# A streaming-encoder block on one core: squares of h reloaded from DRAM, second-product loads ahead of the last stores, next x through four buffers

## Chip, cores and metric

The kernel runs on one core of one Trainium2 chip. The metric is the device time in microseconds (us) of one execution; the time of a kernel is the median of its runs.

## The reference

One layer on x of 2048 rows and 1024 columns, all in float32:

```python
hn   = rmsnorm(h, norm_mix_w)                 # h = x
proj = hn @ w_in                              # 1024 x 4112: q, k, v, z, xbc, dt
h    = h + concat[attention(q,k,v), ssd(z,xbc,dt)] @ w_out
hn   = rmsnorm(h, norm_mlp_w)
h    = h + square(relu(hn @ w_ff1)) @ w_ff2   # D_FF = 4096
y    = rmsnorm(h, norm_final_w)
# ssd: silu(causal conv of xbc), dt = softplus(dt_raw + dt_bias), chunked scan
# of the heads with decay exp(cumsum(-exp(a_log) * dt)), gate silu(z), grouped rmsnorm
```

## The kernel before, in words

The columns of the transposed activations are rows of the sequence. They are worked through in two **halves** of 1024, the first half (`hf` 0) from projection to output, then the second. Every float32 product is made of three matmuls of rounded halves (`mm3`, L245): a tile is split by ACT into a rounded high part (L229) and by DVE into the rest (L230); high x high, high x low and low x high are added in PSUM.

A half goes through these stages:

- **Input projection**, in units of the list `gm` (class `Gemms`, L62): unit dt (L347, 16 columns with the small weight tile `wd`), the convolution units conv0, conv1, ... (24 column blocks by `in_proj`, L332), z, q, k, v. `dt_chain` (L825) turns dt into the decays: eight transposes on PE (L831), `dt_u` (L833), a series on DVE (L843 to L850), `at` (L855), and then, in a second step, a matmul over `at` (L859).
- **SSD scan and attention**, with projection units as filler.
- **Output projection**: units `u_wo_y` (L513), then the four units `u_wo_a` (L534), called **woa** here. Each has 48 matmuls for two of the eight 128-row blocks d. Its reader adds the product to h (L556), forms from two blocks the seven sums and differences of the Strassen-Winograd scheme (`xB11`, `xT1`, `xT2`, `xB22`, `xT3`, `xB21`, `xT4`, L558 to L574), each as a high and a low tile, stores h to `h_d` in DRAM, and squares h on ACT in halves of 512 columns, which DVE adds up in `hacc` (L577 to L583).
- **ff1** (L624): 16 steps mp; each has seven products P1 to P7 of 12 matmuls, named in the order `ORD1` = P1, P6, P5, P7, P2, P3, P4. Step mp 0 first does three quarters (`range(3)`) of the first four products. The weights of a step are loaded, combined (`sum_a`, L587) and split by `Step1` (L598). The reader squares the result and stores seven sums to `f_d` (L680).
- **ff2** (L684): 28 products q of 48 matmuls (the order `ORD2` = P5, P6, P3, ...). `load_w` loads blocks A11, A21, A22, A12 of the weights (1 MB each), `load_a` sums of `f_d`; `split_w` and `split_a` combine and split them. The last products' outputs are scaled with the row norms by `last_rows` (L1065), whose DVE part is 16 operations at L1078.
- **Next half** (L1213 to L1240, `hf` 0 only): the eight blocks of the other half's x are loaded (L178), scaled by `rx` (L1222) and split (L1223); then `load_wd`, the dt unit, the norm rows, conv0, the first step of `dt_chain`, conv1.

**What sets the order.** PE runs in program order, as the code emits its matmuls. On the other engines a scheduler orders the instructions. SP issues all large DMAs, one after the other, and waits at an issue until its tile is free or its data are there; what stands behind it waits too. `stream` (L175, tiles `strm`) and `w_load` (L232, tiles `wraw`) have two buffers each:

```python
t   = wp.tile(list(shape), F, name=name, tag="strm", bufs=2)
raw = wp.tile([P, 8, P], F, name="wraw", tag="wraw", bufs=2)
```

In the rows, `mf` is the PSUM tile of woa and ff2, `fb` that of ff1, `mm` and `mw` those of the input projection, `sB` that of small sums; `w` and `w2h`/`wl` are split weights of ff1 and ff2, `ah`/`al` the split sums of ff2, `st` the tile that is stored to `f_d`.

Of the kernel before, what the change touches and what calls it, by code (L numbers as in the profile page):

```python
# [58 lines left out]
FREED = (6, 0, 2, 1, 4, 5, 7, 3)  # L59
# [91 lines left out]
def hymba(ctx, tc, xT, win, wdt, wout, w1, w2, par, rel, out):  # L151
# [382 lines left out]
    def u_wo_a(s, dd):  # L534

        def fn(wh, wl):
            hs_, X = [], {n: (s.X[n][0][:, dd, :], s.X[n][1][:, dd, :]) for n in s.X}

            def tmp(name):
                return s.mp.tile([P, 512], F, name=name, tag="xt", bufs=6)  # L540
# [3 lines left out]
            for z in range(2):  # L544
# [10 lines left out]
                for b in (1, 0) if z else (0, 1):  # L555
                    dve.tensor_tensor(hx[:, bsl(b)], p_[:, b, :], hx[:, bsl(b)], op=ALU.add)  # L556
# [30 lines left out]
    def sum_a(n, o, v):  # L587
# [4 lines left out]
        o = {"S1": o, "S2": v.get("S1"), "S3": v["A21"], "S4": v.get("S2")}[n]  # L592
# [3 lines left out]
    class Step1:  # L596
# [13 lines left out]
        def split(self, n):  # L610
            if n[0] == "S":
                sum_a(n, self.s.fw.tile([P, 512], F, name="s1", tag="s1", bufs=2) if n == "S1" else None, self.v)
            if n not in self.t:
                self.tile(n)
            split(*parts(self.t[n]), self.v[n])
# [8 lines left out]
    def ff1(s, w, nw):  # L624

        for mp in range(16):
# [25 lines left out]
            for k, p in enumerate(ORD1):  # L652
# [23 lines left out]
                else:  # L676
                    dve.tensor_tensor(a21, b, u, op=ALU.add)
                    square(a21, a21)
                    dve.tensor_tensor(t4, a21, t2, op=ALU.subtract)
            sp.dma_start(f_d[s.hf, mp // 4, :, :, mp % 4, :].rearrange("i p n -> p i n"), st[:, 0:7, :])  # L680
            w, nw = nw, nnw
            yield mp

    def ff2(s):  # L684
# [4 lines left out]
        def load_w(c, n):  # L689
# [3 lines left out]
            sp.dma_start(vs[c][n], w2[c, BLK.index(n)])  # L693

        def split_w(q):
            if q < len(order):
                c, p = order[q]
                n = PA[p]
                if n[0] == "S":
                    sum_a(n, s.f2.tile([P, 4, 512], F, name="ws", tag="ws", bufs=1) if n == "S1" else None, vs[c])  # L700
                lo = s.f2.tile([P, 4, 512], R, name="wl", tag="wl", bufs=2)
                his = [w_tile("w2h").rearrange("p (a b) c -> p a (b c)", a=2) for _ in range(2)]
                for g in range(2):
                    dps = slice(2 * g, 2 * g + 2)
                    split(his[g], lo[:, dps, :], vs[c][n][:, dps, :])
                ws[q] = his, lo

        def load_a(q):
            if q < len(order):
                c, p = order[q]  # L710
                t = s.f2.tile([P, 4, 512], R, name="al", tag="al", bufs=3)
                sp.dma_start(t.bitcast(F), f_d[s.hf, c, SUMS[PB[p]]])
                aa[q] = [None, t]

        def split_a(q):
            if q < len(order):
                aa[q][0] = s.f2.tile([P, 4, 512], R, name="ah", tag="ah", bufs=2)
                split(*aa[q], aa[q][1].bitcast(F))
# [5 lines left out]
        for n in ("A11", "A21", "A22", "A12"):  # L724
            load_w(0, n)
            if n == "A11":
                load_a(0)
        split_w(0)
        split_a(0)
        load_a(1)  # L730
        bank = {}
        for q, (c, p) in enumerate(order):
# [5 lines left out]
            if c < 3:  # L738
                for n in {0: BLK[:1], 3: BLK[1:2], 5: BLK[2:]}.get(k, ()):
                    load_w(c + 1, n)  # L740
            ah, al = aa[q]
            for g in range(2):
# [4 lines left out]
                for z in range(2):  # L747
                    for _ in mm3(b[:, z, :], [(wh[:, z, bsl(j, P)], wl[:, z, bsl(j, P)], ah[:, j, :], al[:, j, :])
                                              for j in range(4)], p not in ON, True, p in ON):
                        pass  # L750
# [332 lines left out]
    def mixer(s):  # L1083
# [38 lines left out]
        s.es_xr, s.xr = open_pool(f"xr{s.hf}", "right")  # L1122
# [5 lines left out]

# [256 lines left out]
```

## Time and profile before

| | |
|---|---|
| time, median of 3 runs | 2803.35 us (2801.03 to 2804.41) |
| profiled execution, its own time | 2804.53 us |
| its span | 2802.8 us |
| PE busy | 2610.8 us (93%), 12398 matmuls |
| DVE busy | 2031.2 us (72%) |
| ACT busy | 1348.3 us (48%) |
| mean granted clock of PE | 0.966 |

The span is what the profiler saw from the first to the last instruction; the rest of the execution's own time lies around it. The clock is a share of full speed, so a stretch at 0.50 runs at 1.2 GHz in place of 2.4 GHz. A timeline row gives the start, the busy time, engine, line and operation, and in brackets how long the engine had been idle and what ended that; `x8` counts merged instructions, whose time is then that of the row together.

### The profile page before, as it was taken

Reading aid. Unit: us, or ns where it says so; the run is one execution under the profiler, and the core shown is the slowest. Engines: PE = TensorE matmul, PEld = TensorE weight load, DVE = VectorE, ACT = ScalarE, POOL = GpSimd, SP = SyncE. Lnnn points to the kernel's source line nnn. Section 1 sums busy time; section 2 is a strip of 40 time slices with the busy share of each in tenths; the row PEclk is TensorE's granted clock in tenths of the full one; section 3 lists DMA queues with packets and bytes.
Section 4 is the critical chain, followed back from the end, with each engine's and each line's share of the span. In section 5 each row is a group of like instructions: output and inputs, shape, how many; then the busy total and the mean of one; then the engine's idle time right before and its main releaser. Section 6 shows DMA issues by size and latency. Waiting matters only on the chain.

```text
span 2802.8 us, 32189 instructions
## 1 busy us (share of the span) xinstructions
PE 2610.8 (93%) x12398; PEld 2137.2 (76%) x12398; DVE 2031.2 (72%) x2866; ACT 1348.3 (48%) x2097; POOL 6.9 (0%) x42
## 2 busy tenths in 40 slices
PE   7999999999799978999599999999997999889997
PEld 4788778788588867888478877887885888668885
DVE  6797777756776646877767887778568666468877
ACT  5565456634554544433336554666335455344332
POOL 0000000000000000000000000000000000000000
PEclk9999999999899998999789999999998999989998
DMA  3232222334354355443332232113343434355432
GB/s 137 87 113 81 97 94 65 115 119 175 136 189 159 142 185 195 174 159 118 105 115 94 87 124 107 55 55 104 110 171 123 164 138 151 137 215 184 161 109 87
DMA packets 121450, 359.98 MB, mean 128 GB/s; under 512 B 10192, under 2 KB 27088, under 8 KB 110032
## 3 DMA queue, kind: packets, MB, share of 16 engines
q1 hardware_dynamic: 121296, 357.93, 36.1%
q8 instruction: 97, 1.59, 0.2%
q14 instruction: 57, 0.47, 0.1%
HBM read 257.09 MB, written 100.79 MB: 128 GB/s over the span
## 4 chain that ended last, share of the span: by engine, by line
PE 81%; DVE 10%; DMA 4%; ACT 2%; issue 1%; SPq 0%; DVEq 0%; ACTq 0%
PE mm L251 25%; PE fb L251 22%; PE mf L251 21%; PE sB L1020 3%; PE mw L251 2%; PE S L977 2%; PE tp L1002 2%; DMA w<-in_w 1%; PE yp L927 1%; PE sB L936 1%; PE yp L925 1%; DMA strm<-h_d 1%; PE mm L356 1%; DMA bias<-in_rel 1%; DVE wlo L230 1%
## 5 line engine op out<-in xcount | busy, mean ns | idle before, releaser
L251 PE MATMUL mm<-x,whi 128*128 128x512 f32 x2304 | 745.1, 405 | 1.4 <-ACT u L372 0.6
L251 PEld LDWEIGHTS mm<-x,whi 128*128 128x128 f32 x2304 | 417.7, 189 | 88.3 <-issue 14.4
L251 PE MATMUL mm<-x,wlo 128*128 128x512 f32 x1152 | 453.1, 393 | 0.0
L251 PE MATMUL mf<-ah,w2h 128*128 128x512 f32 x896 | 351.3, 392 | 47.7 <-ACT w2h L229 47.7
L251 PE MATMUL mf<-ah,wl 128*128 128x512 f32 x896 | 351.1, 392 | 2.3 <-DVE wl L230 2.3
L251 PE MATMUL mf<-al,w2h 128*128 128x512 f32 x896 | 351.0, 392 | 1.9 <-DVE al L230 1.9
L251 PEld LDWEIGHTS mm<-x,wlo 128*128 128x128 f32 x1152 | 217.3, 189 | 48.2
L251 PEld LDWEIGHTS mf<-ah,w2h 128*128 128x128 f32 x896 | 169.7, 189 | 83.6 <-ACT w2h L229 48.6
L251 PEld LDWEIGHTS mf<-ah,wl 128*128 128x128 f32 x896 | 169.4, 189 | 39.1 <-DVE wl L230 3.7
L251 PEld LDWEIGHTS mf<-al,w2h 128*128 128x128 f32 x896 | 169.7, 189 | 38.1 <-DVE al L230 2.7
L988 ACT ACTIVATE pt<-pt,mx 128x640 f32<-128x640 f32 (+4 forms) x128 | 97.6, 762 | 161.7 <-DVE mx L986 161.1
L229 ACT ACTIVATE ah<-al 128x2048 fp32r<-128x2048 f32 x56 | 106.8, 1908 | 132.6 <-PE mf L251 103.6
L230 DVE TENSOR_TENSOR al<-al,ah 128x2048 fp32r<-128x2048 f32 x56 | 127.9, 2284 | 39.5 <-ACT ah L229 39.5
L229 ACT ACTIVATE w<-wraw 128x512 fp32r<-128x512 f32 x128 | 80.2, 630 | 149.7 <-PE fb L251 142.4
L229 ACT ACTIVATE whi<-wraw 128x1024 fp32r<-128x1024 f32 x88 | 92.8, 1054 | 120.0 <-PE mm L251 86.8
L230 DVE TENSOR_TENSOR wlo<-wraw,whi 128x1024 fp32r<-128x1024 f32 x88 | 107.5, 1222 | 45.5 <-ACT whi L229 40.7
L251 PE MATMUL fb<-xT2h,w 128*128 128x512 f32 x256 | 87.3, 401 | 35.7 <-ACT w L229 35.7
L230 DVE TENSOR_TENSOR w<-s,w 128x512 fp32r<-128x512 f32 x96 | 66.1, 689 | 70.0 <-ACT w L229 68.9
L760 DVE TENSOR_TENSOR acc<-mf,acc 128x1024 f32<-128x1024 f32 x64 | 77.9, 1219 | 53.1 <-PE mf L251 52.9
L986 DVE CUSTOM_DVE_ANT_0 pt<-S,bias 128x640 f32<-128x640 f32 (+4 forms) x128 | 94.1, 735 | 30.4 <-PE S L977 29.8
L892 ACT ACTIVATE csb<-csb,cst 128x128 f32<-128x128 f32 x256 | 79.2, 389 | 70.1 <-DMA csb<-cs_d 70.1
L229 ACT ACTIVATE w2h<-w 128x1024 fp32r<-128x1024 f32 x64 | 65.3, 1054 | 92.3 <-PE mf L251 80.1
(297 smaller groups left out, 5316.6 us busy)
## 6 DMA issues: line engine op xcount, KB each, us to landing
f_d<-st SPq DMA_DIRECT2D x32, 1792.0 KB, 6.2
al<-f_d SPq DMA_DIRECT2D x56, 1024.0 KB, 4.8
wraw<-in_win SPq DMA_DIRECT2D x64, 512.0 KB, 3.3
wraw<-in_w SPq DMA_DIRECT2D x64, 512.0 KB, 3.2
w<-in_w SPq DMA_DIRECT2D x32, 1024.0 KB, 4.8
strm<-in_xT SPq DMA_DIRECT2D x32, 512.0 KB, 4.4
csb<-cs_d SPq DMA_DIRECT2D x32, 512.0 KB, 3.9
h_d<-strm SPq DMA_DIRECT2D x32, 512.0 KB, 2.6
```

The source lines that it names most:

```text
L229: act.activation(hi, raw, AF.Copy)
L230: dve.tensor_tensor(lo, raw, hi.bitcast(F), op=ALU.subtract)
L251: pe.matmul(ps, a, b, start=(first and i == 0), stop=(last and i == n - 1), skip_group_check=on)
L356: pe.matmul(ps[b][:48, pc], s.wd[:, kt, :], x_[kt][:, c], start=(kt == 0 and x_ is s.xh), stop=(kt == NKT - 1 and x_ is s.xl))
L760: dve.tensor_tensor(o, b, o, op=ALU.add)
L892: act.activation(E[:, h, :], E[:, h, :], AF.Relu, scale=-1.0, bias=s.cst[:, k:k + 1])
L925: pe.matmul(yo[:, j, :], S[:, bsl(j, P)], Cf[:, ch], start=True, stop=True)
L977: pe.matmul(S[:, a, 0:w], q[p][hd][:, bsl(lb, P)], s.ks[p][hd][:, k0 + st:k0 + st + w], start=(z == 0), stop=(z == 1))
L986: dve.tensor_tensor_reduce(out=o_, in0=s_, in1=b_, scale=1.0, scalar=1e30, op0=ALU.add, op1=ALU.min, accum_out=mx)
L988: act.activation(pt[:, 0:n], pt[:, 0:n], AF.Exp, scale=-1.0, bias=mx, accum_out=sm)
L1002: pe.transpose(tp[:, bsl(c, P)], pt[:, bsl(c, P)], ident)
L1020: pe.matmul(pv[:, i0 * P:(i1 + 1) * P], lhsT, rhs, start=(z == 0), stop=(z == 2 * len(order) - 1))
```

## The change

1. **Squares of h.** woa no longer squares h. In ff1, steps mp 0 to 3 reload two blocks of `h_d` each through `stream`; ACT squares 128x1024, DVE adds up in `ra` (`squares_of`). The mean and the row norms move from mp 0 to mp 5 and 6, the next half's x squares from one block in each of mp 4 to 11 to two in each of mp 7 to 10, `rx` from mp 13 to 12. The addition to h (L556) is one 128x1024 operation except in the last block.
2. **First weights of ff1.** Four of the seven `step`s of the first `Step1` are emitted ahead of the end of woa, three just behind it; one tile `s1` in place of two; temporaries of woa 5 in place of 6; all seven sums in one pool on the left.
3. **First loads of ff2.** They are emitted in mp 15 of ff1 ahead of its last store to `f_d` (the pool of ff2 is opened there). The first product's loads, sums, splits and matmuls are done in two halves along the contraction.
4. **Next half.** Odd blocks of x come through `wraw`, even ones through `strm`; `load_wd` and the first splits of conv0's weights are emitted during ff2. The dt unit, conv0 and conv1 are woven: for each block of x two dt matmuls, three of conv0, three of conv1, for both groups of 512 columns in turn (`weave(3)`). `dt_chain` starts behind conv1.

```diff
 def u_wo_a(s, dd):                                  # woa
-                for b in (1, 0) if z else (0, 1):
-                    dve.tensor_tensor(hx[:, bsl(b)], p_[:, b, :], hx[:, bsl(b)], op=ALU.add)
+                for b in (1, 0) if d == 7 else (slice(0, 2),):
+                    o = hx.rearrange("p (a b) -> p a b", a=2)[:, b]
+                    dve.tensor_tensor(o, p_[:, b], o, op=ALU.add)
...
-                for b in range(2):
-                    c = bsl(b)
-                    if d == 0:
-                        act.activation(s.hacc[:, c], hx[:, c], AF.Square)
-                    else:
-                        sq = tmp("hsq")
-                        act.activation(sq, hx[:, c], AF.Square)
-                        dve.tensor_tensor(s.hacc[:, c], s.hacc[:, c], sq, op=ALU.add)
 def ff1(s, w, nw):
+            yield mp
             sp.dma_start(f_d[s.hf, mp // 4, :, :, mp % 4, :].rearrange("i p n -> p i n"), st[:, 0:7, :])
             w, nw = nw, nnw
-            yield mp
 def ff2(s):
-        for n in ("A11", "A21", "A22", "A12"):
-            load_w(0, n)
-            if n == "A11":
-                load_a(0)
...
+        for h in (slice(0, 2), slice(2, 4)):
+            load_w(0, "A21", h)
+            load_w(0, "A22", h)
+            load_a(0, h)
+        load_w(0, "A11")
+        load_w(0, "A12")
         split_w(0)
         split_a(0)
         load_a(1)
+        yield
...
+                for js in (range(4),) if q else (range(2), range(2, 4)):
+                    for z in range(2):
 def mlp(s):
         w.load(1)
+        for k in range(4):
+            w.step(k)
         until(s, "woa")
+        for k in range(4, 7):
+            w.step(k)
+            if k in (4, 6):
+                nw.load(k // 6)
...
+        def squares_of(src, kt):
+
+            hx = stream(src)
+            act.activation(hx if kt else ra, hx, AF.Square)
+            if kt:
+                dve.tensor_tensor(ra, ra, hx, op=ALU.add)
+
         for mp in ff1(s, w, nw):
-            if mp == 0:
-                means(sums_f(s, s.hacc), s.v)
+            if mp < 4:
+                for kt in (2 * mp, 2 * mp + 1):
+                    squares_of(h_d[s.hf, kt], kt)
+            elif mp == 5:
+                means(sums_f(s, ra), s.v)
...
+            elif mp == 15:
+
+                s.es_xx.close()
+                s.es_g, s.f2 = open_pool(f"f2{s.hf}", "left")
+                products = ff2(s)
+                next(products)
...
             for kt in range(NKT):
-                xr = stream(xT[kt * P:(kt + 1) * P, TH:2 * TH])
+                src = xT[kt * P:(kt + 1) * P, TH:2 * TH]
+                xr = w_load(src.rearrange("p (a b) -> p a b", b=P)).rearrange("p a b -> p (a b)") if kt % 2 else stream(src)
...
-            for _ in range(NKT):
-                gm.step()
+            products = gm.weave(3)
+            for _ in range(NKT + 1):
+                next(products)
             for r in rows:
                 next(r)
-            until(n, "dt")
+            for _ in products:
+                pass
             for r in rows:
                 for _ in r:
                     pass
-            gm.hold()
             n.chain = dt_chain(n)
             next(n.chain)
-            gm.hold()
```

**DVE at the end of woa, first half.** Before, from the last unit's first addition to h (L556) to the first combined weights of ff1 (L593; `w` and `s` with numbers are weight tiles, `t` and `b` temporaries):

```order
811 L556 TENSOR_TENSOR strm<-mf,strm 128x512 x2
812 L560 TENSOR_TENSOR t_5964<-strm 128x512
813 L556 TENSOR_TENSOR strm<-mf,strm 128x512 x2
814 L267 SCALAR_TENSOR_TENSOR xB11l<-strm,pr,xB11h 128x512
815 L583 TENSOR_TENSOR v<-v,hsq 128x512 x2
...
820 L583 TENSOR_TENSOR v<-v,hsq 128x512 x2
821 L230 TENSOR_TENSOR xT2l<-t_6005,xT2h 128x512
822 L570 SCALAR_TENSOR_TENSOR b_6004<-strm,pr,b_6004 128x512
...
825 L230 TENSOR_TENSOR xT4l<-t_6005,xT4h 128x512
826 L593 TENSOR_TENSOR s_6039<-wraw 128x512
827 L593 TENSOR_TENSOR wraw<-wraw 128x512
828 L230 TENSOR_TENSOR w_6041<-s_6039,w_6041 128x512
```

With the change (L558 is the addition to h, L587 the weights' sums, L1200 the sum of squares), from the second-to-last unit's end:

```order
813 L230 TENSOR_TENSOR xT4l<-t_5872,xT4h 128x512
814 L230 TENSOR_TENSOR w_5998<-wraw,w_5998 128x512
815 L230 TENSOR_TENSOR w_6054<-wraw,w_6054 128x512
816 L558 TENSOR_TENSOR strm<-mf,strm 128x1024
817 L558 TENSOR_TENSOR strm<-mf,strm 128x512 x2
818 L562 TENSOR_TENSOR t_5938<-strm 128x512
...
820 L587 TENSOR_TENSOR s_6066<-wraw 128x512
...
824 L587 TENSOR_TENSOR wraw<-wraw 128x512
...
829 L230 TENSOR_TENSOR xT3l<-b_5972,xT3h 128x512
830 L230 TENSOR_TENSOR xT4l<-t_5973,xT4h 128x512
831 L1200 TENSOR_TENSOR ra<-ra,strm 128x1024
832 L656 TENSOR_TENSOR u<-fb,u 128x512
```

The additions of squares are gone from the unit, and the first weights' sums and splits stand inside and ahead of it; the first sum of squares comes directly behind it, ahead of the first reader of ff1 (`u`).

**SP from ff1 to ff2, first half.** Before (`w` with a number is a weight block of ff2, `in_win` weights of the second half's projection):

```order
200 L680 DMA f_d<-st 128x7x512
201 L178 DMA strm<-h_d 128x1024
202 L234 DMA wraw<-in_win 128x1024 x2
203 L680 DMA f_d<-st 128x7x512 x2
204 L693 DMA w_8326<-in_w 128x2048
205 L712 DMA al<-f_d 128x2048
206 L693 DMA w_8330<-in_w 128x2048
207 L693 DMA w_8332<-in_w 128x2048
```

With the change:

```order
205 L675 DMA f_d<-st 128x7x512
...
208 L675 DMA f_d<-st 128x7x512
209 L689 DMA w_8291<-in_w 128x1024
210 L689 DMA w_8292<-in_w 128x1024
211 L724 DMA al<-f_d 128x1024
212 L689 DMA w_8291<-in_w 128x1024
213 L689 DMA w_8292<-in_w 128x1024
214 L724 DMA al<-f_d 128x1024
215 L689 DMA w_8294<-in_w 128x2048
216 L689 DMA w_8295<-in_w 128x2048
217 L724 DMA al<-f_d 128x2048
218 L675 DMA f_d<-st 128x7x512
```

Six half loads for the first product, two weight loads and the load of `al` for the second product now stand ahead of the last store of `st`, where all of ff2's loads stood behind it.

**PE from the first half to the second.** Before (`wd` dt weights, `accu` sums of squares of the output, `dg` norm rows, `mw` conv0 and conv1):

```order
4341 L251 MATMUL mf<-ah,wl 128x512
4342 L356 MATMUL mm<-x,wd 48x512 x16
4343 L294 MATMUL sB<-ones,accu 128x1 x16
4344 L356 MATMUL mm<-x,wd 48x512 x16
4345 L316 MATMUL sB<-dg,ones 128x512 x2
4346 L251 MATMUL mw<-x,whi 128x512 x2
4347 L251 MATMUL mw<-x,wlo 128x512
...
4378 L831 MATMUL sB<-ident,dtr 128x16 x8
4379 L251 MATMUL mw<-x,whi 128x512 x2
```

With the change:

```order
4341 L251 MATMUL mf<-ah,wl 128x512
4342 L356 MATMUL mm<-x,wd 48x512 x2
4343 L251 MATMUL mw<-x,whi 128x512 x2
4344 L251 MATMUL mw<-x,wlo 128x512
4345 L251 MATMUL mw<-x,whi 128x512 x2
4346 L251 MATMUL mw<-x,wlo 128x512
...
4382 L294 MATMUL sB<-ones,accu 128x1 x16
4383 L356 MATMUL mm<-x,wd 48x512 x2
4384 L251 MATMUL mw<-x,whi 128x512 x2
...
4422 L251 MATMUL mw<-x,wlo 128x512
4423 L316 MATMUL sB<-dg,ones 128x512 x2
4424 L858 MATMUL sB<-ident,dtr 128x16 x8
4425 L251 MATMUL mm<-x,whi 128x512 x2
```

The dt matmuls lie among those of conv0 and conv1; the norm rows (`dg`) and dt's transposes (`ident,dtr`) stand behind both, directly ahead of the next unit, conv2 (`mm`).

## Rows read from the trace of the kernel before

**Rows 1.** Waits of PE, whole span: engine line <- releaser, us in total, times, longest us.
```profile
PE mf L251 <- ACT w2h L229: 47.7, 2, 23.9
PE mm L356 <- DVE wd L225: 37.5, 1, 37.5
PE fb L251 <- ACT w L229: 35.7, 2, 17.9
```

**Rows 2.** Timeline of PE, woa to ff1, first half: start, us, instruction [idle before].
```profile
702.80 0.40 PE L251 MATMUL fb<-xB11h,w 128*128 128x512 f32 x1
720.93 0.80 PE L251 MATMUL fb<-xT2h,w 128*128 128x512 f32 x1 [17.73 <-ACT w L229]
```

**Rows 3.** Timeline of DVE, same stretch.
```profile
705.19 1.29 DVE L556 TENSOR_TENSOR strm<-mf,strm 128x512 f32<-128x512 f32 x2 [1.64 <-DMA strm<-h_d]
...
708.98 1.29 DVE L583 TENSOR_TENSOR v<-v,hsq 128x512 f32<-128x512 f32 x2
...
716.68 0.69 DVE L230 TENSOR_TENSOR xT4l<-t,xT4h 128x512 fp32r<-128x512 f32 x1
...
720.90 0.69 DVE L230 TENSOR_TENSOR w<-s,w 128x512 fp32r<-128x512 f32 x1 [0.76 <-ACT w L229]
```

**Rows 4.** Windows there: us, busy by engine (count), PEclk, DMA share, GB/s.
```profile
703.20:720.93 17.73, 0.00 (x1) 0.01 (x1) 15.16 (x25) 8.37 (x15) 0.00 (x0) 0.63 0.28 111
720.93:724.60 3.67, 3.67 (x9) 2.88 (x10) 3.52 (x6) 2.14 (x4) 0.00 (x0) 0.50 0.38 128
724.60:740.00 15.40, 15.40 (x68) 12.60 (x67) 9.81 (x16) 7.88 (x14) 0.00 (x0) 0.99 0.22 74
```

**Rows 5.** The page's part 5, ACT 128x1024, and part 6, load of a strm tile.
```profile
L229 ACT ACTIVATE whi<-wraw 128x1024 fp32r<-128x1024 f32 x88 | 92.8, 1054 | 120.0 <-PE mm L251 86.8
...
strm<-in_xT SPq DMA_DIRECT2D x32, 512.0 KB, 4.4
```

**Rows 6.** Timeline of PE, ff1 to ff2, first half.
```profile
1033.62 0.40 PE L251 MATMUL fb<-xT4h,w 128*128 128x512 f32 x1
1057.89 0.79 PE L251 MATMUL mf<-ah,w2h 128*128 128x512 f32 x1 [23.87 <-ACT w2h L229]
...
1060.26 0.79 PE L251 MATMUL mf<-ah,wl 128*128 128x512 f32 x1 [1.15 <-DVE wl L230]
```

**Rows 7.** Timeline of the SP queue, same stretch: when SP issued.
```profile
1019.48 18.12 SPq L680 DMA_DIRECT2D f_d<-st  x2
1037.65 0.55 SPq L693 DMA_DIRECT2D w<-in_w  x1
```

**Rows 8.** Timeline of DVE, same stretch.
```profile
1036.51 0.69 DVE L679 TENSOR_TENSOR st<-st 128x512 f32<-128x512 f32 x1 [0.76 <-ACT st L650]
```

**Rows 9.** Windows there.
```profile
1040.00:1050.00 10.00, 0.00 (x0) 0.00 (x0) 0.00 (x0) 0.59 (x1) 0.00 (x0) 0.50 1.02 385
...
1060.00:1066.00 6.00, 5.74 (x14) 4.48 (x15) 5.97 (x5) 3.27 (x3) 0.00 (x0) 0.50 0.57 238
```

**Rows 10.** Timeline of PE, from the first half to the second.
```profile
1405.90 6.14 PE L356 MATMUL mm<-x,wd 128*48 128x512 f32 x16 [37.51 <-DVE wd L225]
...
1422.25 1.88 PE L316 MATMUL sB<-dg,ones 128*128 128x512 f32 x4
```

**Rows 11.** Timeline of the SP queue, same stretch.
```profile
1369.93 26.99 SPq L178 DMA_DIRECT2D strm<-in_xT  x8
```

**Rows 12.** Timeline of DVE, same stretch.
```profile
1400.90 1.23 DVE L1222 TENSOR_TENSOR strm<-strm,rx 128x1024 f32<-128x1024 f32 x1 [1.34 <-DMA strm<-in_xT]
...
1423.87 10.62 DVE L1078 SCALAR_TENSOR_TENSOR acc<-acc,pr,sB 128x512 f32<-128x512 f32 x16
1435.68 0.29 DVE L833 COPY dt_u<-sB 128x128 f32<-128x128 f32 x1 [1.18 <-PE sB L831]
...
1456.20 0.28 DVE L855 TENSOR_TENSOR at<-dtt,nega 128x128 f32<-128x128 f32 x1
```

**Rows 13.** Window there.
```profile
1411.00:1421.50 10.50, 10.50 (x50) 7.44 (x49) 4.46 (x19) 2.37 (x4) 0.00 (x0) 0.67 0.00 0
```

More of the change, by code (lines that the diff above doesn't have):

```diff
@@ L692, in load_w, with tile_s, tile_wl @@
                                                              dict(tag="ra", bufs=3)))
-            sp.dma_start(vs[c][n], w2[c, BLK.index(n)])
+        def load_w(c, n, dps=slice(0, 4)):
+            sp.dma_start(vs[c][n][:, dps, :], w2[c, BLK.index(n)][:, dps, :])
+        def tile_s(c):
+            vs[c]["S1"] = s.f2.tile([P, 4, 512], F, name="ws", tag="ws", bufs=1)
+        def tile_wl(q):
+            ws[q] = ([w_tile("w2h").rearrange("p (a b) c -> p a (b c)", a=2) for _ in range(2)],
+                     s.f2.tile([P, 4, 512], R, name="wl", tag="wl", bufs=2))
         def split_w(q):
@@ L698, in split_w @@
                 n = PA[p]
[L699 to L702, printed above, removed]
+                if q:
+                    if n == "S1":
+                        tile_s(c)
+                    tile_wl(q)
+                his, lo = ws[q]
@@ L703, in split_w, with tile_a @@
                 for g in range(2):
                     dps = slice(2 * g, 2 * g + 2)
+                    if n[0] == "S" and (g == 0 or q == 0):
+                        v = {m: t[:, dps, :] if q == 0 else t for m, t in vs[c].items()}
+                        sum_a(n, v.get(n), v)
+                        if q:
+                            vs[c][n] = v[n]
                     split(his[g], lo[:, dps, :], vs[c][n][:, dps, :])
-                ws[q] = his, lo
-        def load_a(q):
+        def tile_a(q):
+            aa[q] = [None, s.f2.tile([P, 4, 512], R, name="al", tag="al", bufs=3)]
@@ L746, in ff2 @@
                 wh, wl = ws[q][0][g], ws[q][1][:, 2 * g:2 * g + 2, :]
[L747 to L750, printed above, removed]
+                for js in (range(4),) if q else (range(2), range(2, 4)):
+                    for z in range(2):
+                        for _ in mm3(b[:, z, :], [(wh[:, z, bsl(j, P)], wl[:, z, bsl(j, P)], ah[:, j, :], al[:, j, :])
+                                                  for j in js], p not in ON and js[0] == 0, js[-1] == 3, p in ON):
+                            pass
                 dps = slice(2 * g, 2 * g + 2)
@@ L1150, in mlp @@
             n = PB[p]
-            s.X[n] = tuple((xx if i == 0 or n in ("B11", "T1", "T2", "T3") else s.xr)
-                           .tile([P, 4, 512], R, name=f"x{n}{'hl'[i]}") for i in range(2))
+            s.X[n] = tuple(xx.tile([P, 4, 512], R, name=f"x{n}{i}") for i in "hl")
         gm.finish(marks[s.hf, "woa"] - 1)
@@ L1204, in mlp @@
         tail = lambda: s.ps.tile([P, 2, 512], F, name="mf", tag="M", bufs=2).rearrange("p a b -> p (a b)")
-        for c, k, p in ff2(s):
+        for c, k, p in products:
+            if s.hf == 0 and (c, k) == (2, 2):
+                load_wd(n)
+            if s.hf == 0 and (c, k) == (3, 6):
+                gm.horizon = len(gm.units)
+                gm.split(gm.at + 1)
             if c == 1 or (c, k) == (2, 0):
```

59 lines of the change are left out of this document (30 added, 29 removed).

## The prediction

> **What bounds the kernel now.** I read the waits of PE first, since PE is busy for 93% of the span. Three waits stand out: the first matmuls of ff2 wait twice, 47.7 us in all, the dt matmuls of the second half once for 37.5, the first products of ff1 twice, 35.7 in all [rows 1]. They lie where one stage ends and the next begins, and make 121 us of 2804. Only at these three places can the change gain much, so I read there the timelines of PE, DVE and SP, and the windows for the clock.
>
> *Into ff1.* PE stops after the matmul at 702.80 and goes on at 720.93 [rows 2]. DVE works without a pause: the last unit of woa starts at 705.19, when its block of h has landed, has two pairs of square sums in it (1.29 us each), and ends with `xT4l` at 717.4; only then come the weights of ff1, and the first split that PE wants is under way at 720.90 [rows 3]. The wait drops the clock (0.63 on average over it), so the next nine matmuls take 3.67 us; at 0.99, 68 take 15.40, or 0.2265 each [rows 4].
>
> *Into ff2.* PE stops at 1034.0, has two matmuls at 1057.89 and goes on at 1060.26 [rows 6]. SP issued the last two stores of ff1 from 1019.48 to 1037.6, for the second one waits for its data, and only then the loads of ff2 [rows 7]. DVE had finished those data at 1037.2 [rows 8]. From 1040 to 1050 the DMA engines are full at 385 GB/s, while PE does nothing; then 14 matmuls run at clock 0.50 [rows 9].
>
> *Into the second half.* PE waits 37.51 us, until 1405.90 [rows 10], while eight blocks of x are loaded through two buffers, issued over 26.99 us [rows 11], and scaled, the last at 1400.90 [rows 12]; `wd` comes after them. Then follow dt, norm rows, conv0, conv1 and conv2, and beside conv0 DVE does the 16 operations on the output rows, 10.62 us from 1423.87, before `dt_u` at 1435.68 and `at` at 1456.20 [rows 12].
>
> **The change, part by part.** Sums are made against the profiled execution, 2804.53 us, which is 1.2 above the median.
>
> *1. Into ff1.* Out of woa go 14 additions of 512 columns per half (0.6 us each where they follow one another), in go 12 operations on the first weights, most of them in the first units. The last unit loses two pairs (2.4 us) and takes on two weight sums (1.2): 12.2 us become 11.0. Its start moves from 705.2 to about 703.2, for the units before it are shorter by about 2 together. So the last X tile is ready at about 714 in place of 717.4, and the weights no longer come after it. PE goes straight on behind woa with 36 matmuls on three quarters of the sums (8.2 us, to 709), and does the rest as X comes; P2, P3 and P4, 36 matmuls, can't start before 714 and end at 722.2. Before, step mp 0 had 75 matmuls left at 720.93: 3.67 us for nine, 66 x 0.2265, end 739.5. Gain 17.3 per half. Against it stand the squares in mp 0 to 3: eight reloads of 512 KB, each 4.4 us to landing, and eight squares of 1.05 on ACT [rows 5], whose queue also splits the weights. The step ahead covers most of it, since a step has 84 x 0.2265 = 19 us and two reloads with two squares take about 11; I take 1.5 us for the splits of mp 1, which stand behind the first squares, with 0 and 5 as bounds. **Net 15.8 per half, 31.6 in all (24 to 35).** The other moves (means, row norms, x squares, `rx`) cost nothing: they shift among steps in which DVE and ACT have room, 9.81 and 7.88 of 15.40 us in the step shown [rows 4].
>
> *2. Into ff2.* The loads now stand ahead of the last store. Behind the store at 1019.48 [rows 7] they wait only for tiles that ff1 has done with: those of `xB11` (free early in mp 15) and of P7's sums (about 1025.5). The first product wants 3 MB, which at 385 GB/s [rows 9] takes 8.2 us, so it is there by about 1037. What is late next is DVE: its last sum of ff1 ends at 1037.2 [rows 8]. Then come the half sum (1.2), ACT's high half (1.05), the split of `al` (1.05 and 1.2): PE starts at about 1041.8. It has stood for 7.8 us, so I let it restart at the low clock and pay 1.8 (nine matmuls in 3.67 in place of 2.04) [rows 4]. The 48 matmuls of the first product end at 1054.5; the second product's `al` stands behind a full weight sum on DVE and is split at about 1057.6. Before, 46 matmuls were left at 1060.26; 14 of them took 6.0 us [rows 9], 32 x 0.2265 more make 1073.5. **Gain 15.8 per half, 31.6 in all (24 to 37).**
>
> A split load moves less at a time. In the rows a 512 KB block takes 4.4 us from issue to landing when its queue is not full [rows 5], and 385 GB/s are reached with 1 MB transfers in flight together [rows 9]; no row shows six halves together. If they ran one after another, six would take 26.4 us and land at about 1046.5, 9 us later per half than I have it. The Trainium skill, "DMA: Bandwidth & Descriptors", section "Measured (HBM→SBUF, 128 partitions, SWDGE, issued from GpSimd)", speaks against the split: it advises batching transfers to 1 MiB or more, as each pays a fixed part of some 2 us. By its fit, an estimate, six halves one by one would take about 19 us in place of 13 for three whole blocks, 6 later per half, and the sum would come to 2757. I forecast the shared rate, since SP issues the next transfer before the last has landed; the 9 us of the rows are a rival below.
>
> *3. Into the second half.* With four buffers the loads no longer wait for DVE; DVE itself needs 8 x 2 x 1.23 us for scaling and, taken alike, splitting, two blocks of it now scaled ahead, so x is ready at about 1392 in place of 1404.6 (1400.90 and two or three such operations). `wd` and conv0's weights are there before. But PE goes block by block through dt, conv0 **and conv1**, and conv1's weights are loaded through `wraw`, whose buffer is held by an odd block of x until about 1389.4. Load (3 to 4.4 [rows 5]), split (1.05 and 1.2): 1394 to 1396. PE therefore waits at the first block until about 1394.5 (26 us; before 37.5). Then it does some 121 matmuls, 32 small sums (4.6) and pays a restart (about 3.5, since the window of the restart before shows 0.67 for 10 us [rows 13]): conv1 ends at about 1430, before at 1446.6 (conv0 began at 1424, 96 x 0.2265).
>
> That lead of 16.6 us is what I think is given back. Before, the rows' 10.62 us on DVE lay beside conv0, and the 20.5 from `dt_u` to `at` beside conv1 and conv2 [rows 12]. Now the norm rows and dt's transposes stand behind conv1, so all of it begins there: matmuls of the rows 1.6, two weight splits 2.4, rows 10.6, then `dt_u` to `at`, which without the ten long operations that lay in between (12 us) takes about 10. So `at` comes 24.6 us behind conv1, at 1454.6 (before 1456.5). PE has conv2 to cover it, which ends 12.5 behind conv1; it waits 12 us. ACT, too, does conv0's activation only behind that chain, and with it conv2's PSUM comes free late: conv3 starts at about 1461.4, before at 1458.1. With a second restart of 2.3 us: **a loss of 5.6 (from a loss of 15, if the chain is woven with conv1's operations as before, to a gain of 12, if the scheduler's order on the chip lets dt ahead of the rows).**
>
> Sum: 31.6 + 31.6 - 5.6 = 57.6 us; 2804.5 - 57.6 = 2746.9, against the median 1.2 less: **2745 us**.
>
> **The rivals.** *A: the second half keeps its lead.* For: x is there 12 us sooner, and the work on PE is the same. Against: rows and chain, 30 us of DVE, have lost the 22 us of matmuls that covered them. With a gain of 12 in place of the loss of 5.6: 2727.
>
> *B: the loads of ff2 are not early.* For: SP waits in order, and if the tile of a weight block is freed only by the last products, or the store of mp 14 lasts, everything behind waits as before. Against: the order on SP, where they stand ahead of the last store. The gain of 31.6 is gone: 2776.
>
> *C: half loads run one by one.* 9 us per half more in part 2: 2763.
>
> *D: the squares hold ff1 up (slower).* ACT's queue is in order: a square that waits for its reload holds the weight splits behind it. If PE's lead in weights (one step) doesn't cover that, each of eight pieces costs 4.4 us of landing and 1.05 [rows 5]: 44 per half, 87 in all, 2832. It decides when two reloads with squares take longer than a step's slack, which from 19 us a step I see at no more than a few us; against it, too, x squares went the same way in mp 4 to 11 before, and PE has no wait of that kind among the first three rows [rows 1].
>
> *E: the change does nothing.* Only the first product of ff2 and the first step of ff1 come sooner, and PE then waits that much longer for the second, whose weights and sums go through the same DVE queue at the old pace: about 2803. Against: over the span DVE is busy 72%, and PE shows no large wait inside ff1 or ff2, where its weights come at that pace [rows 1].
>
> **How the numbers follow.** Forecast 0.50, A 0.22, B 0.13, C 0.07, D 0.04, E 0.04. All but D and E are faster by over 0.2% (5.6 us, about what a measurement can tell from no change): faster 0.92, same 0.04, slower 0.04. The range leaves out D, E, the lower end of A and the upper half of B: 2720 to 2776.
>
> **What would show it.** Waits of PE: ff1's fall from 17.9 each to a few of 2; ff2's from 23.9 to about 8, and a second of 2 to 3 ahead of the second product; the dt wait of 37.5 becomes three: 26 at the first conv1 matmul, 12 at the matmul over `at`, some 6 at conv3. SP issues weight loads of ff2 before 1030 minus what ff1 gained. If PE waits in ff1 for `w` in mp 1 to 4, D is at work; if the wait into ff2 stays over 20, B; if conv3 starts over 10 us sooner behind the first half's last product than now, A.

## The result and the profile after

The changed kernel takes 2755.89 us (median of 4 runs, 2752.51 to 2758.92), before 2802.73 (4 runs): a ratio of 0.9833, 95% interval 0.9816 to 0.985. That is 46.8 us faster; forecast were 58 faster, 2745 with a range of 2720 to 2776. The profiled execution took 2756.40 us with a span of 2754.7, PE's mean clock went from 0.966 to 0.975, and its busy time is the same (2611.8 us, before 2610.8). On balance, then, the gain is idle time of PE that is gone; inside the busy time some 5 us of faster matmuls in ff1 (last section) make up for more matmuls at the low clock (75 us of busy time at 0.50, before 68).

The waits of PE in the changed kernel (columns as in [rows 1]):

```profile
PE mw L251 <- ACT whi L229: 15.8, 1, 15.8
PE mf L251 <- ACT ah L229: 12.9, 2, 6.5
...
PE mm L356 <- ACT x L266: 9.1, 3, 6.0
PE fb L251 <- ACT u L654: 8.8, 2, 4.8
...
PE mf L251 <- DVE al L230: 8.3, 6, 2.8
PE mm L251 <- ACT u L372: 8.2, 3, 5.8
...
PE sB L858 <- DVE acc L1105: 5.3, 1, 5.3
...
PE sB L886 <- DVE at L882: 3.4, 1, 3.4
```

The three large waits of [rows 1], 47.7 + 37.5 + 35.7, are replaced by many: 12.9 + 8.3 into ff2, 8.8 and some 4 on `xT2l` into ff1, and into the second half 15.8 + 5.3 + 3.4, 7.6 of the 8.2, and at the dt matmuls 6.0 of the 9.1 and 2.5 on `x` from DVE. Into the second half PE thus waits 40.7 us in all, more than the 37.5 before. The same in the timeline of PE, first half, where [rows 2], [rows 6] and [rows 10] stood:

```profile
712.75 0.50 PE L251 MATMUL fb<-xT2l,w 128*128 128x512 f32 x1 [1.90 <-DVE xT2l L230]
...
720.37 0.80 PE L251 MATMUL fb<-xB21h,w 128*128 128x512 f32 x1 [4.83 <-ACT u L654]
...
1028.47 0.80 PE L251 MATMUL mf<-ah,w2h 128*128 128x512 f32 x1 [6.47 <-ACT ah L229]
...
1045.82 0.80 PE L251 MATMUL mf<-al,w2h 128*128 128x512 f32 x1 [2.14 <-DVE al L230]
...
1348.31 0.66 PE L356 MATMUL mm<-x,wd 128*48 128x512 f32 x1 [6.04 <-ACT x L266]
1351.43 0.66 PE L356 MATMUL mm<-x,wd 128*48 128x512 f32 x1 [2.45 <-DVE x L267]
...
1369.21 1.22 PE L251 MATMUL mw<-x,whi 128*128 128x512 f32 x2 [15.84 <-ACT whi L229]
...
1410.62 1.00 PE L858 MATMUL sB<-ident,dtr 16*128 16x16 f32 x8 [5.34 <-DVE acc L1105]
...
1427.44 0.49 PE L886 MATMUL sB<-at,tri 128*128 128x128 f32 x2 [3.38 <-DVE at L882]
...
1433.93 1.22 PE L251 MATMUL mm<-x,whi 128*128 128x512 f32 x2 [5.78 <-ACT u L372]
```

From the first and last matmuls of each stage in this timeline and in that of the kernel before, the lengths in us:

| stretch on PE | before | after | gain | forecast |
|---|---|---|---|---|
| first ff1, from the end of woa | 333.1 | 320.4 | 12.7 | 15.8 |
| second ff1 | 332.2 | 318.4 | 13.8 | 15.8 |
| first ff2, from the end of ff1 | 334.4 | 320.3 | 14.1 | 15.8 |
| second ff2 | 334.7 | 319.3 | 15.4 | 15.8 |
| end of ff2 to the fill of projections behind conv3 | 137.0 | 143.1 | -6.1 | -5.6 |
| from there to the second woa | 559.8 | 561.5 | -1.8 | 0 |

The rest, of both signs, lies ahead of the first woa and behind the last product. So each place went the way that was forecast, and most of what is missing lies in ff1.

**Into ff1.** X is complete at 715.4 (714 forecast). Then PE waits, not for X nor for weights but for `u`, ACT's copy of P1 (L654), into whose bank P2 goes on adding. The timeline of ACT shows what stands ahead of `u`:

```profile
714.05 0.63 ACT L229 ACTIVATE xT4h<-t 128x512 fp32r<-128x512 f32 x1
716.87 1.06 ACT L1198 ACTIVATE ra<-strm 128x1024 f32<-128x1024 f32 x1 [2.19 <-DMA strm<-h_d]
718.64 1.06 ACT L1198 ACTIVATE strm<-strm 128x1024 f32<-128x1024 f32 x1 [0.71 <-DMA strm<-h_d]
719.72 0.60 ACT L654 ACTIVATE u<-fb 128x512 f32<-128x512 f32 x1
```

Two squares, each waiting for its block of h from DRAM, hold a copy whose input was there since 710.6. The windows there (columns as in [rows 4]):

```profile
715.50:720.37 4.87, 0.04 (x2) 0.01 (x1) 0.65 (x1) 2.77 (x4) 0.00 (x0) 0.76 0.66 253
720.37:724.80 4.43, 4.43 (x10) 3.48 (x11) 4.43 (x7) 1.52 (x2) 0.00 (x0) 0.50 0.40 135
```

The clock falls in the wait, and the next ten matmuls take 4.43 us in place of 2.3.

**Into ff2.** SP, where [rows 7] stood, and DVE at the same place:

```profile
1007.14 0.38 SPq L675 DMA_DIRECT2D f_d<-st  x1
1007.61 1.69 SPq L689 DMA_DIRECT2D w<-in_w  x2
1013.87 0.33 SPq L724 DMA_DIRECT2D al<-f_d  x1
...
1025.27 0.38 SPq L675 DMA_DIRECT2D f_d<-st  x1
```

```profile
1024.55 0.69 DVE L673 TENSOR_TENSOR st<-st 128x512 f32<-128x512 f32 x1 [0.76 <-ACT st L644]
1025.16 1.22 DVE L587 TENSOR_TENSOR ws<-w,w 128x1024 f32<-128x1024 f32 x1
1027.50 1.22 DVE L230 TENSOR_TENSOR wl<-ws,w2h 128x1024 fp32r<-128x1024 f32 x1 [1.12 <-ACT w2h L229]
...
1405.12 5.36 DVE L1105 SCALAR_TENSOR_TENSOR acc<-acc,pr,sB 128x512 f32<-128x512 f32 x8
...
1411.53 5.35 DVE L1105 SCALAR_TENSOR_TENSOR acc<-acc,pr,sB 128x512 f32<-128x512 f32 x8
1416.80 0.28 DVE L860 COPY dt_u<-sB 128x128 f32<-128x128 f32 x1
...
1427.10 0.28 DVE L882 TENSOR_TENSOR at<-dtt,nega 128x128 f32<-128x128 f32 x1
```

The first loads are issued from 1007.61, ahead of the last store at 1025.27, and the half sum (1025.16) follows directly on DVE's last work for ff1, as forecast. PE stands for 6.47 us (7.8 forecast), and again for 2.14 at the second product. While the loads are in flight the window reads (columns as in [rows 4]):

```profile
1012.00:1024.00 12.00, 9.99 (x45) 7.93 (x43) 3.81 (x5) 4.50 (x8) 0.00 (x0) 1.00 1.01 363
```

**Into the second half.** The lower four of the rows of DVE above answer to [rows 12]: 16 operations on the rows from 1405.12, `dt_u` at 1416.80, `at` at 1427.10. ff2 ended at 1342.3, the last matmul of conv1 at 1403.6, 61.3 us later (61.6 forecast; the 60.5 in the expectation of e2_turns_old below is the same distance, read 0.8 short); `at` is done 23.8 behind conv1 (24.6), conv3 starts 30.4 behind it (31.4). One detail I had not seen: dt's transposes wait 5.34 us for a PSUM tile that the rows hold, so conv2 starts late and the wait at `at` is the smaller for it, 5.3 + 3.4 where I had 12.

### The profile page after: what moved, and what is told of

It reads as the page before. It is cut to its first block, busy times and chain, and to the rows that moved or that the text cites. A ratio compares the mean times of both kernels' runs of the same rounds, so it can differ in the third digit from the quotient of the medians.

```text
span 2754.7 us, 32168 instructions
## 1 busy us (share of the span) xinstructions
PE 2611.8 (95%) x12398; PEld 2138.8 (78%) x12398; DVE 2025.4 (74%) x2842; ACT 1345.1 (49%) x2083; POOL 7.0 (0%) x42
## 4 chain that ended last, share of the span: by engine, by line
PE 80%; DVE 11%; DMA 3%; ACT 3%; issue 2%; SPq 0%; DVEq 0%; ACTq 0%
PE mm L251 25%; PE fb L251 21%; PE mf L251 21%; PE sB L1047 2%; PE mw L251 2%; PE S L1004 2%; PE tp L1029 2%; DMA strm<-h_d 1%; PE yp L954 1%; PE sB L963 1%; PE yp L952 1%; DVE acc L1105 1%; DVE wlo L230 1%; DVE pt L1013 1%; DVE pl L1033 1%
## 5 line engine op out<-in xcount | busy, mean ns | idle before, releaser
L251 PE MATMUL mf<-ah,w2h 128*128 128x512 f32 x896 | 351.6, 392 | 12.9 <-ACT ah L229 12.9
L251 PEld LDWEIGHTS mf<-ah,w2h 128*128 128x128 f32 x896 | 169.8, 189 | 49.2 <-ACT ah L229 13.8
L229 ACT ACTIVATE ah<-al 128x2048 fp32r<-128x2048 f32 (+1 forms) x58 | 107.0, 1848 | 107.9 <-PE mf L251 105.9
L230 DVE TENSOR_TENSOR al<-al,ah 128x2048 fp32r<-128x2048 f32 (+1 forms) x58 | 128.3, 2212 | 12.3 <-ACT ah L229 12.3
L1013 DVE CUSTOM_DVE_ANT_0 pt<-S,bias 128x640 f32<-128x640 f32 (+4 forms) x128 | 94.2, 736 | 31.4 <-PE S L1004 30.9
L1033 DVE TENSOR_TENSOR pl<-tp,ph 128x640 fp32r<-128x640 f32 (+4 forms) x128 | 94.0, 735 | 22.2 <-ACT ph L1032 20.8
```

The lines of the kernel that those rows point to most:

```text
L229: act.activation(hi, raw, AF.Copy)
L230: dve.tensor_tensor(lo, raw, hi.bitcast(F), op=ALU.subtract)
L251: pe.matmul(ps, a, b, start=(first and i == 0), stop=(last and i == n - 1), skip_group_check=on)
L1013: dve.tensor_tensor_reduce(out=o_, in0=s_, in1=b_, scale=1.0, scalar=1e30, op0=ALU.add, op1=ALU.min, accum_out=mx)
L1033: dve.tensor_tensor(ol, tp[:, 0:n], oh.bitcast(F), op=ALU.subtract)
```

## Experiments

Each was timed beside the kernel before, whose medians there were 2803.5, 2802.7 and 2802.0. Ratios are to it, with 95% intervals. The length of a stage whose code is untouched differs from run to run too: one ff2 takes 317.6 to 321.0 us in the runs that have it as changed.

**e1_pinned: squares behind their step.** The changed kernel, with

```diff
-            act.activation(hx if kt else ra, hx, AF.Square)
+            tc.keep_in_program_order(act.activation(hx if kt else ra, hx, AF.Square))
```

> The changed kernel with one difference: each square of h is pinned on ACT behind the work of its own ff1 step, so that the copy of P1 (u, which P2 waits for) no longer stands behind the first two squares in mp 0. Theory (ACT in order): in the changed kernel P2 of mp 0 waits 4.83 us for u and restarts at the low clock (about 1.8 us more); both go, in both halves, so about 2756 - 13 = 2743 us, and PE waits for u fall from 8.8 us to under 1. Rival (X tiles or weights are late there anyway, u is only the last of several): the wait is renamed and the time stays at 2753 to 2757.

Measured: 2744.96 us, 0.9789 (0.9775 to 0.9803), 11 us faster than the changed kernel. No wait of ff1 for `u` is left, and ff1 takes 313.0 and 310.9 us in place of 320.4 and 318.4. So one copy behind two squares cost 7.4 us per half: the wait of 4.8 (4.0 in the second half), the restart of about 2.2, and little more for the other squares. `squares_of` also does the squares of the next x, so the edit pins those too; the second half has none, and gains as much. Of the 14.9 us some 2 are lost again at the start of the second half (145.2 us to the fill behind conv3, 143.1 in the changed kernel); what is left of the difference to the medians' 11 is less than the 9 us over which the four runs of this kernel spread.

**e3_squares_woa: squares back in woa.** The changed kernel, with the removed lines of L577 to L583 put back (into `v`), `means` in mp 0, the row norms in mp 2 and no `squares_of(h_d...)`.

> The changed kernel with the squares of h back in woa as before (ACT squares of 512 columns, DVE sums, means in mp 0, no reload in ff1), everything else as changed, first weights of ff1 early. Theory (what ends the wait into ff1 is that the weights come early; the squares' move itself gains 2 to 3 us in woa and loses more in mp 0): X is complete about 2.5 us later, but P2 does not wait for u: 2 to 5 us faster per half, 2746 to 2752. Rival (the squares' move is what shortens the wait): slower by 5 to 10 us per half, 2766 to 2776.

Measured: 2757.26 us, 0.9832 (0.9819 to 0.9846): neither. The wait for `u` is gone, others stand in its place:

```profile
PE fb L251 <- ACT xT2h L229: 6.8, 2, 3.7
...
PE fb L251 <- DVE strm L558: 5.0, 2, 2.5
```

ff1 takes 322.5 and 321.3 us, 2 to 3 more than with the squares moved and 10 more than with them moved and pinned. The move is worth some 10 us per half, and the order on ACT took three quarters of it back. That the weights' steps are emitted early seems to be worth little, though no run takes it out alone: e5_onepool below, which emits them late, has an ff1 of 323.3 and 322.6.

**e5_onepool: the kernel before with all X tiles in one pool.** Nothing else of the change but the room that it needs:

```diff
-            s.X[n] = tuple((xx if i == 0 or n in ("B11", "T1", "T2", "T3") else s.xr)
-                           .tile([P, 4, 512], R, name=f"x{n}{'hl'[i]}") for i in range(2))
+            s.X[n] = tuple(xx.tile([P, 4, 512], R, name=f"x{n}{i}") for i in "hl")
...
-                return s.mp.tile([P, 512], F, name=name, tag="xt", bufs=6)
+                return s.mp.tile([P, 512], F, name=name, tag="xt", bufs=5)
...
-                sum_a(n, self.s.fw.tile([P, 512], F, name="s1", tag="s1", bufs=2) if n == "S1" else None, self.v)
+                sum_a(n, self.s.vp.tile([P, 512], F, name="s1", tag="s1", bufs=1) if n == "S1" else None, self.v)
```

> The kernel before with one difference: all fourteen X tiles lie in one pool on the left (and for the room, the temporaries of woa 5 in place of 6, one tile s1). ff2 is emitted where it was, behind the last store of ff1, and its loads are whole. Theory now (the loads are late because their tiles overlap ones that ff1 frees last, not because of where they are emitted): SP issues the first loads ahead of the last store, the wait into ff2 falls from 23.9 to 12 to 15 us, 16 to 24 us faster than before in all, about 2783. Rival (the place in the code decides, as the prediction had it): the wait stays at 23.9 and the time at 2800 to 2806.

Measured: 2752.43 us, 0.9816 (0.9803 to 0.983), 51 us faster than before, 31 more than the theory had, and no slower than the whole change. Waits of PE:

```profile
PE mf L251 <- ACT w2h L229: 20.0, 2, 10.0
...
PE fb L251 <- DVE strm L556: 11.2, 2, 6.0
```

The wait into ff2 is 10.0 in place of 23.9, though no load was emitted earlier; the wait into ff1 is down as well, which I had not expected of this run. It contains two edits of place, so the next two take them apart.

**e6_s1only** has of e5_onepool only the lines on `s1` and `xt`, **e6_xpool** only those on X and `xt`.

> The kernel before with one difference: the temporary s1 of the first weights' sums lies in one tile of the pool vp in place of two in the pool ff (and, for the room, woa's temporaries have 5 buffers in place of 6). Where the steps of the first weights are emitted stays as before. Theory (the first weights were late because s1's tile became free only when woa's pool was closed): the wait into ff1 falls as in e5_onepool, from 17.9 to about 9 with its parts, and ff1's end comes 9.7 us sooner per half; the wait into ff2 stays at 23.9: 2803.5 - 19.4 = 2784 us. Rival (the single pool of X does both): 2800 to 2806.

> The kernel before with one difference: all fourteen X tiles in one pool on the left (and woa's temporaries 5 in place of 6); s1 stays in two tiles of ff. Theory: the counterpart of e6_s1only: the wait into ff1 stays at 17.9, the wait into ff2 falls from 23.9 to about 10, ff2 ends 13.3 to 14.2 us sooner per half: 2803.5 - 27.5 = 2776 us. With e6_s1only the two gains add up to that of e5_onepool (51 us, of which some 3 lie elsewhere). Rival (they overlap, or one needs the other): the sum of both is under 40.

Measured: 2786.97 (0.9946, 0.9934 to 0.9959) and 2766.68 (0.9866, 0.9851 to 0.988), 15.8 and 36.1 us faster than before, together 51.9, the 51 of e5_onepool. Waits of PE with s1 moved, then with X moved:

```profile
PE mf L251 <- ACT w2h L229: 47.8, 2, 23.9
...
PE fb L251 <- DVE strm L556: 9.6, 2, 5.0
```

```profile
PE fb L251 <- ACT w L229: 35.1, 2, 17.6
PE mf L251 <- ACT w2h L229: 20.0, 2, 10.0
```

Each edit shortens one wait and leaves the other as it was [rows 1]. The pool brought 8.6 us more than expected: the two ff2 gain 15.5 and 13.7 us, but ff1 gains 2.3 and 3.1 as well, with its wait unchanged (see the last section). With the temporary alone moved, the scheduler puts the first weights' sums into woa (at 708.31 on DVE, ahead of the last unit's addition at 710.99); with the pool alone, it puts the loads of ff2 ahead of the last store, as SP shows there:

```profile
1020.13 0.55 SPq L693 DMA_DIRECT2D w<-in_w  x1
...
1037.14 0.37 SPq L680 DMA_DIRECT2D f_d<-st  x1
```

Both are emitted where they were before, so the place of the tiles decides, and not the place in the code. Which tile's release they had been waiting for was not read from a row. woa's 5 temporaries are in both runs, and each run leaves the other's wait as it was, so they account for neither.

**e4_ff2_whole: ff2's opening as before.** The changed kernel with `yield mp` behind the store again, the pool of ff2 opened after the loop, whole loads and whole products.

> The changed kernel with ff2's opening as before: loads emitted behind the last store and whole, the first product not in halves; the X tiles stay in one pool. SP's order has the first loads ahead of the last store all the same. Theory (the pool brings the early loads, the halves only a little): the wait into ff2 is 10.0 us in place of 6.5 and the second product follows with less waiting, ff2's end 1 us later per half: 2756 to 2760. Rival (the emission ahead of the store carries the gain of this place, as the prediction had it): 29.5 us slower, 2785.

Measured: 2757.02 us, 0.9838 (0.9824 to 0.9851), within the spread of the changed kernel. Its wait is longer,

```profile
PE mf L251 <- ACT w2h L229: 20.0, 2, 10.0
```

(6.5 twice with the halves), but the first ff2 takes 320.4 us as against 320.3. What the halves gain at the first product is lost at the second, where PE waits for `al` 8.3 us in all with the halves and 2.3 without. The second ff2 takes 321.1 as against 319.2, which is no more than that stage differs between runs.

**e2_turns_old: dt, rows, conv0, dt chain, conv1 in turn again**, with four buffers for x:

```diff
-            products = gm.weave(3)
-            for _ in range(NKT + 1):
-                next(products)
+            for _ in range(NKT):
+                gm.step()
             for r in rows:
                 next(r)
-            for _ in products:
-                pass
+            until(n, "dt")
             for r in rows:
                 for _ in r:
                     pass
+            gm.hold()
             n.chain = dt_chain(n)
             next(n.chain)
+            gm.hold()
```

> The changed kernel with the turns at the start of the second half as before (dt for all blocks, norm rows, conv0, first step of the dt chain, conv1), x still through four buffers. Theory (the weave gives its lead back because rows and dt chain stand behind conv1): conv1 ends 63 to 65 us behind ff2 in place of 60.5, but dt_u and at run beside conv1 and conv2, and conv3 follows conv2 without the waits of 5.3, 3.4 and 5.8 us: 14 to 18 us faster, 2738 to 2742 us. Rival (the early lead is what counts and the chain would be as late anyway): no faster, 2755 to 2762 us.

Measured: 2732.24 us, 0.9744 (0.973 to 0.9757), 23.7 us faster than the changed kernel, more than expected. conv1 ends 61.8 us behind ff2, 0.5 later than with the weave, and then nothing waits: from ff2's end to the fill behind conv3 it takes 120.6 us in place of 143.1. DVE and PE in this run:

```profile
1380.81 10.62 DVE L1105 SCALAR_TENSOR_TENSOR acc<-acc,pr,sB 128x512 f32<-128x512 f32 x16
1392.62 0.29 DVE L860 COPY dt_u<-sB 128x128 f32<-128x128 f32 x1 [1.19 <-PE sB L858]
...
1410.87 0.29 DVE L882 TENSOR_TENSOR at<-dtt,nega 128x128 f32<-128x128 f32 x1
```

```profile
1414.43 0.38 PE L886 MATMUL sB<-at,tri 128*128 128x128 f32 x2
```

The rows run beside conv0, the chain beside conv1 and conv2, and the matmul over `at` has no wait in its row. The weave's lead is 0.5 us, and in e1_pinned and e3_squares_woa, with the same weave, conv1 comes later than here (62.3 and 65.1 us); I had expected 3 to 5. That is part of why the gain is larger. The rest is in the waits behind conv1, 16.3 us with one of 1.8 that I had not counted, the low clock behind them, and the scan (559.4 us as against 561.5).

**e9_twobuf: as e2_turns_old, x through `strm` alone** (`xr = stream(src)`).

> e2_turns_old with x through the two strm buffers alone, as before. Theory (the four buffers bring the x sooner, and the old turns keep that): the wait ahead of dt is 37 to 39 us in all again, 13 to 17 us slower than e2_turns_old's 2732, so 2745 to 2749. Rival (what is gained in e2_turns_old comes from wd and conv0's weights being loaded during ff2): within 4 us of 2732.

Measured: 2745.94 us, 0.98 (0.9787 to 0.9814), 13.7 us slower than e2_turns_old: what the four buffers are worth. The time is the one expected, but not the wait: up to conv0 PE waits 28.6 us in all, 16.2 in e2_turns_old and 38.3 in e5_onepool, and not 37 to 39. So two causes share this place. Of the 22 us less waiting some 12 belong to the buffers, and 10 to something that e9_twobuf has kept; `wd` and conv0's weights, loaded during ff2, are the likely one, which no run takes out alone.

**e7_best: e1_pinned and e2_turns_old together.**

> The changed kernel with both e1_pinned (squares of h behind the work of their step on ACT) and e2_turns_old (dt, rows, conv0, dt chain, conv1 in turn). If the two causes are apart, their gains add up: 2732.2 - 11 = 2721 us (2716 to 2726). If they share a cover, 2728 or more.

Measured: 2717.05 us, 0.9694 (0.9681 to 0.9706), the fastest version found, 39 us under the changed kernel. Against e2_turns_old it gains 15.2: ff1 gives 5.9 and 6.7, and the remaining 2.6 lie in stages that the two edits leave alone. With the old turns nothing is lost at the start of the second half (120.2 us to the fill behind conv3, 120.6 in e2_turns_old). Of the range expected, 2716 to 2726, it is the lower end.

**e8_weave2: e1_pinned, with only dt and conv0 woven**, then the rows, conv1, the dt chain.

> As e1_pinned, but the weave at the start of the second half takes dt and conv0 alone; then the norm rows, conv1, and only then the dt chain's transposes. Theory (the weave itself is sound, what hurt was conv1 in it, which left nothing to cover the rows): PE has conv1 (11 us) beside the rows' 10.6 us on DVE and conv2 beside the dt chain, and no longer waits 15 us for conv1's weights with x at hand: conv1 ends about 50 to 53 us behind ff2 (61.6 with the old turns), 5 to 10 us faster than e7_best, 2711 to 2716. Rival (the dt chain comes later than with the old turns by as much, since its transposes stand behind conv1): a wait of about 10 us at the matmul over at, and 2718 to 2726, no better than e7_best.

Measured: 2724.17 us, 0.9717 (0.9704 to 0.973). conv1 ends 53 us behind ff2, as expected, but the rival holds, with a smaller wait than its 10 us; its row on PE:

```profile
1405.68 0.79 PE L886 MATMUL sB<-at,tri 128*128 128x128 f32 x2 [6.38 <-DVE at L882]
```

**e10_chain_first: as e8_weave2, the dt chain ahead of the rows on DVE**, its transposes in a tile of tag `mm` ahead of conv1.

> As e8_weave2, but dt's transposes go into a PSUM tile of tag mm and stand ahead of conv1, and DVE does the dt chain before 14 of the 16 operations on the output rows. Theory (in e8_weave2 the rows on DVE, 10.6 us, hold dt_u and at, and with them the matmul over at): at is ready about 54 us behind ff2's end and the wait of 6.4 us there goes; conv3 begins at about 70 us (78 in e7_best): 2705 to 2714 us. Rival (the rows then hold conv0's own operations on DVE, and with them ACT and the PSUM of conv2): the wait moves to conv3 and the time stays at 2716 to 2724.

Measured: 2726.53 us, 0.9736 (0.9723 to 0.975). `at` is ready 53 us behind ff2 and its wait is gone, but

```profile
1396.29 0.38 PE L886 MATMUL sB<-at,tri 128*128 128x128 f32 x2
...
1408.54 1.22 PE L251 MATMUL mm<-x,whi 128*128 128x512 f32 x2 [11.64 <-ACT u L372]
```

conv3 now waits 11.64 us, longer than the wait that went, and the time is above the ranges of theory and rival. The wait is where the rival had it, but not for its cause. The rows' 14 operations on DVE (9.30 us from 1384.92) are over at 1394.2; ACT is later:

```profile
1396.26 1.06 ACT L229 ACTIVATE whi<-wraw 128x1024 fp32r<-128x1024 f32 x1 [9.82 <-PE mm L251]
```

ACT stands at the weight split of a later unit until PE is done with conv2. Only behind it come the copies of conv0 out of PSUM, whose matmuls had ended by 1372, then conv0's operations on DVE (7.26 us from 1400.84), and behind those the copies that free conv2's PSUM, at 1407.90. As with `u`, copies whose input is there stand behind an operation that waits. What pinning that split would give was not tried, and that this stretch can't be shorter than in e7_best isn't shown.

## Why the prediction was right, and where it was not

- **What bounds the kernel** was right: only the three places moved, by 26.5 us in ff1 (some 5 of them a faster pace, last section), 29.5 in ff2, and -7.9 from the second half's start to its woa.
- **Part 1, net 15.8 per half, measured 12.7 and 13.8.** The term that was mis-sized is the price of the squares. "I take 1.5 us for the splits of mp 1" looked at the weight splits behind the squares; what stood behind them was the copy of P1, for which PE waits in the same step. It cost 7.4 per half (e1_pinned). The gross gain of 17.3 was right: 17.3 less 7.4, and 2.5 that ff1's later steps gained from the pool, make 12.4. But 7.0 of it per half come from the place of `s1` with no line of the order changed (e6_s1only), where I had the early emission of the steps. That ACT is a queue in order was rival D's mechanism; it came true at one copy, and not at eight pieces.
- **Part 2, 15.8 per half, measured 14.1 and 15.4.** The chain of steps held: loads ahead of the store, DVE's last sum next, a second wait ahead of the second product. Two things in it were off. I let the gain come from where the loads are emitted; it comes from the pool of the X tiles (e6_xpool, e4_ff2_whole). That the size came out is in part luck: the change held the pool as well, and I had given it no price. And for the second wait I priced no restart, though the clock fell there too.
- **Part 3, a loss of 5.6, measured 6.1, and 1.8 more in the scan.** The best of the three: conv1's end, `at` and conv3 came within 0.3, 0.8 and 1.0 us of their forecast distances, and e2_turns_old shows that the cause was the cover lost. The wait at `at` was 12 in the forecast and came as 5.3 and 3.4, with 1.8 more behind conv3. The further 1.8 us in the scan need not belong to the change: that stretch takes 558.8 to 562.8 us in the runs here, 558.8 in e3_squares_woa with the weave and 561.8 in e9_twobuf without.
- **Rivals.** A (the lead is kept) and B (loads not early) are out by the profile. C, half loads one by one, is out too: with them in flight the DMA engines moved 363 GB/s from 1012 to 1024, and the six halves landed 1.2 to 2.3 us apart, the last at 1024.28, not 4.4 apart; DVE found its first halves there when it came. The Trainium skill, "DMA: Bandwidth & Descriptors", section "Measured (HBM→SBUF, 128 partitions, SWDGE, issued from GpSimd)", advises batches of 1 MiB or more. The 6 us per half that the prediction worked out from that page's fit did not come: with several loads in flight on SP's queue, halves cost no time here that can be told from none (2755.89 us as against 2757.02 in e4_ff2_whole), and brought none. E is out.

## What to carry to other kernels

A load or a first computation that comes late at a stage's border may wait for the place of a tile, not for its turn in the code: try the pools first, here two edits of placement gave 51 us, as much as the whole change with its two losses in it (e7_best, without them, has 35 more). When work is moved onto an engine with an ordered queue, ask for every instruction that will stand behind it, who waits for that one, in the same step above all. And before matmuls are moved ahead, list what ran beside them: the weave brought conv1 forward by 0.5 us at most and uncovered 22 us of work on DVE (from 1405.12 to 1427.38).

## What the hardware showed that I had not expected

Short waits bring the low clock too, but not all of them. The windows of the changed kernel:

```profile
712.75:715.50 2.75, 2.52 (x8) 1.34 (x8) 2.62 (x4) 1.26 (x2) 0.00 (x0) 1.00 0.35 103
...
1035.20:1043.60 8.40, 8.40 (x37) 6.71 (x35) 7.24 (x6) 4.83 (x5) 0.00 (x0) 0.98 0.46 192
...
1045.82:1049.00 3.18, 3.18 (x8) 2.50 (x9) 2.22 (x2) 3.18 (x4) 0.00 (x0) 0.50 0.49 206
```

Behind the wait of 1.90 us at 712.75 the matmuls run at 1.00; behind that of 2.14 at 1045.82 eight take 3.18 us at 0.50, some 1.4 more than at full clock. Ahead of the first wait PE had run without a pause at full clock for over 50 us (1.00 from 657.60 to 710.85); ahead of the second for 8.4 us, and before those 6.7 at 0.50. Two waits show no more than that both outcomes occur.

Where a tile lies changes the pace of the matmuls that read it. From the same step of the second ff1 to its end, the kernel before, then e6_xpool:

```profile
2190.97:2441.26 250.29, 250.29 (x1094) 204.88 (x1093) 160.20 (x237) 121.28 (x200) 0.00 (x0) 1.00 0.39 142
```

```profile
2173.39:2421.17 247.78, 247.78 (x1094) 204.93 (x1093) 159.48 (x237) 121.41 (x200) 0.00 (x0) 1.00 0.44 160
```

The work is the same, no wait lies in it, and the clock is the same, but it takes 250.29 and 247.78 us (250.28 in e6_s1only). By the starts in the timeline of PE, a matmul on `xB21`, `xB22` and `xT4`, whose low tiles lay in the pool on the right, comes on average 231 to 232 ns behind the last one in the kernel before, one on the four others 227 to 228; with all in one pool on the left it is 227 for all seven, and so it is in the changed kernel. This is where ff1's 2.3 and 3.1 us in e6_xpool come from. What on the right slows them was not tried.
